# A mixing step on VectorE, late affine work on GpSimd, and the first step of each norm, in a two-block transformer kernel

## The chip, the cores and the metric

The kernel runs on one core of a Trainium2 chip, in one launch. The metric is the device time of the launch in microseconds (us), as the median of several runs; the time before is 1526.29 us. Inputs, weights and outputs are float32 in the chip's main memory.

The engines are called by short names: PE (matmuls), DVE (the vector engine), ACT (the scalar engine), POOL (GpSimd) and SP (used here for its queue of transfers).

## The reference

256 tokens of width 1024 pass two blocks. The part on which the change acts most is layer A of the first block:

```
proj = h @ w_in                       # 1024 -> 2 x 2048
u, gate = proj[..., :2048], proj[..., 2048:]
for g, w in enumerate((2, 4, 8, 16)): # 512 channels each
    cs = cumsum(u of group g over tokens)
    pooled = (cs - shifted(cs, w)) / min(pos + 1, w) - u of group g
    mixed = pooled @ w_grp[g]
y = (mixed * scale * silu(gate)) @ w_out
h = layer_norm(h * ALPHA + y) * ln_g + ln_b
```

Layer B of the same block makes keys and values from h, attends within dilated windows with 16 heads, gates, projects, and ends in a second layer norm. The second block has two layers, each with a token mixer and an MLP; each half ends with an rms norm of its output, a gated addition to the stream, and an rms norm of the stream for the next half, whose shift and scale come from a conditioning vector.

## The kernel before

**Products.** A float32 product is done as three PE matmuls on parts that were rounded to a narrower format: high by high, high by low, low by high (`mm3`, lines 178 to 183). Weights come in tiles of 512 KB (`stream`, L120 to L132): the SP queue loads `ws` (four buffers), ACT rounds it to the high part `wh` (L128), DVE subtracts to get the low part `wl` (L130); five buffers each. The activations are split in the same way by `split` (ACT L135, DVE L136). Tiles of activations hold features on the partitions and tokens along the row.

**Order.** The order of the matmuls on PE is written out by hand, with side work (`tick`, `weave`) put between the main ones; products for the conditioning (L268) serve as filling. On DVE, ACT, POOL and SP the order is set by a scheduler from priorities, in which later code comes later, and code under `high_priority(100)` is put ahead. Each engine then runs its own list strictly in that order.

**Layer A** (`layer_a`, L422 on). The tokens are transposed on PE (L432), then for each group of 512 channels, windows 16, 8, 4, 2 in turn, and for each half of a group (two feature tiles of 128): PE makes u; ACT copies it out (L457); DVE adds shifted copies, one to four times, to get the sum over the window (L462, tiles `wa` and `wb`); POOL multiplies by 1 / count (L465, constant `inv`) and subtracts u (L466); ACT and DVE split the result; then PE makes the gate half, and ACT and DVE its silu (L471, L472). The group's own product (`grp`, L493) stands one group behind. The output product follows (`out_mm`), and the two token tiles' layer norms: statistics on DVE (L539 to L542), `rstd`, normalising on DVE (L548). The normalised tiles are transposed on PE (`tile_T`, L377) and scaled while they are taken out (`hT_evac`, L400, L402).

**rstd** (L159 to L170) makes 1 / sqrt: a DVE step `v` (L164, or L166 in rms norms), then POOL's power (L169), which alone is under `high_priority(100)`. The rms norms end with DVE multiplying by it (L717 in `rms_tile`, L1075 in `residual`; L1071 and L1072 are the squares on ACT and the multiplication by the gate on DVE before it).

**The affine step.** The stream itself still needs ln_g and ln_b of layer A: eight POOL operations of 128x512 on `xt` in place (L604), for which `layer_b` keeps a list; two are given out behind each block of columns of layer B's values, six blocks (`cb`) in all, whose results are copied out of PSUM by DVE (L594) and ACT. They have no dependence on the values, so that they stand in POOL's list as soon as `xt` can be written, which is when the transposes have read it.

**Set-up** (L313 on). SP loads the identity, the two token tiles (128x1024 each, L323) and the first weights; DVE clears constants, among them S (L344).

## Time and profile before

| | before |
|---|---|
| median of 3 runs | 1526.29 us (1524.75 to 1528.28) |
| the profiled execution | 1525.75 us |
| its span | 1524.0 us |
| mean granted PE clock | 0.99 of full speed |
| busy: PE, DVE, ACT, POOL | 1469.2, 924.6, 721.2, 172.8 us |
| moved by DMA | 241.80 MB, 159 GB/s |

The span runs from the first to the last instruction; the 1.75 us between it and the execution's time lie outside. Engines run side by side, and each waits only where a tile is not yet there or not yet free. A share of busy time is an average over stages; what a wait costs is read where it stands, from the engine that has no work in hand. In the rows a `<-` behind an idle time names the instruction, or the transfer, that ended it.

### The profile page before, as it was taken

The page shows a single profiled execution, that of the slowest core. Times are in us where ns is not written, and L with a number is a line of the kernel's source. Part 1 is how long each engine was busy: PE and PEld are TensorE (multiplying, and loading weights), DVE is VectorE, ACT ScalarE, POOL GpSimd, SP SyncE. Part 2 cuts the span into 40 slices and gives each one's busy share as a digit, 9 for nine tenths or more (in the row PEclk, how much of TensorE's full clock was granted, in tenths as well). Part 3 has the DMA queues.
Part 4 walks back from the last instruction along what each step waited for, and adds up shares of the span by engine and source line. Part 5 has one row for each costly group of instructions (what it writes and reads, how often), then busy time and mean ns, then how long its engine had stood idle before and what let it go on. Part 6 is the DMA issues. An engine that isn't in the chain of part 4 may idle for free.

```text
span 1524.0 us, 23366 instructions
## 1 busy us (share of the span) xinstructions
PE 1469.2 (96%) x8966; PEld 1213.7 (80%) x8966; DVE 924.6 (61%) x1660; ACT 721.2 (47%) x1397; POOL 172.8 (11%) x240
## 2 busy tenths in 40 slices
PE   8899899999999999999899999999998999899998
PEld 8898678888999677776787777777886886599986
DVE  5676755657677877658774243433448687665554
ACT  4454444445466546645663232221426466555443
POOL 4431300000010142001100000000001220000000
PEclk9999999999999999999999999999999999999999
DMA  8568576867554722114434445343344255645562
GB/s 305 179 194 261 162 233 189 249 198 230 171 178 155 261 84 84 32 39 131 135 109 138 138 154 164 119 150 107 96 151 125 85 139 180 221 153 191 184 191 84
DMA packets 186544, 241.80 MB, mean 159 GB/s; under 512 B 15296, under 2 KB 132080, under 8 KB 186368
## 3 DMA queue, kind: packets, MB, share of 16 engines
q1 hardware_dynamic: 185168, 237.11, 49.4%
q0 software_dynamic: 1264, 3.19, 0.6%
q8 instruction: 70, 1.15, 0.3%
q14 instruction: 42, 0.34, 0.1%
HBM read 239.19 MB, written 2.03 MB: 158 GB/s over the span
## 4 chain that ended last, share of the span: by engine, by line
PE 68%; DVE 9%; POOL 4%; ACT 3%; issue 3%; DMA 1%; SPq 0%; POOLq 0%; DVEq 0%; ACTq 0%
PE ps L181 20%; PE ps L182 19%; PE ps L183 19%; POOL sm L169 2%; DVE wl L130 2%; PE ps L958 2%; PE ps L874 2%; PE ps L268 2%; PE ps L940 1%; PE ps L700 1%; PE ps L687 1%; POOL t L753 1%; DVE fm L136 1%; DVE sm L919 1%; PE ps L665 1%
## 5 line engine op out<-in xcount | busy, mean ns | idle before, releaser
L130 DVE TENSOR_TENSOR wl<-ws,wh 128x1024 fp32r<-128x1024 f32 x336 | 413.7, 1233 | 357.5 <-ACT wh L128 347.2
L128 ACT CAST wh<-ws 128x1024 fp32r<-128x1024 f32 x336 | 351.2, 1049 | 398.5 <-PE ps L183 211.7
L181 PE MATMUL ps<-fm,wh 128*128 128x256 f32 (+1 forms) x1416 | 428.2, 302 | 4.2 <-ACT fm L135 4.2
L183 PE MATMUL ps<-fm,wl 128*128 128x256 f32 (+1 forms) x1416 | 421.8, 298 | 5.0 <-DVE wl L130 4.9
L182 PE MATMUL ps<-fm,wh 128*128 128x256 f32 (+1 forms) x1416 | 421.6, 298 | 0.3 <-DVE fm L136 0.3
L182 PE MATMUL ps<-wl,fm 128*128 128x512 f32 (+1 forms) x912 | 355.6, 390 | 10.5 <-DVE wl L130 10.5
L181 PE MATMUL ps<-wh,fm 128*128 128x512 f32 (+1 forms) x912 | 364.0, 399 | 0.3 <-ACT fm L135 0.3
L183 PE MATMUL ps<-wh,fm 128*128 128x512 f32 (+1 forms) x912 | 354.8, 389 | 2.5 <-DVE fm L136 2.5
L181 PEld LDWEIGHTS ps<-fm,wh 128*128 128x128 f32 x1416 | 267.7, 189 | 30.5 <-issue 10.9
L183 PEld LDWEIGHTS ps<-fm,wl 128*128 128x128 f32 x1416 | 267.7, 189 | 15.6 <-DVE wl L130 6.7
L182 PEld LDWEIGHTS ps<-fm,wh 128*128 128x128 f32 x1416 | 267.6, 189 | 9.8 <-DVE fm L136 0.7
L181 PEld LDWEIGHTS ps<-wh,fm 128*128 128x128 f32 x912 | 172.4, 189 | 58.7 <-issue 17.7
L182 PEld LDWEIGHTS ps<-wl,fm 128*128 128x128 f32 x912 | 172.8, 189 | 48.3 <-DVE wl L130 14.0
L183 PEld LDWEIGHTS ps<-wh,fm 128*128 128x128 f32 x912 | 172.2, 189 | 42.7 <-DVE fm L136 4.2
L135 ACT CAST fm<-t 128x128 fp32r<-128x128 f32 (+2 forms) x232 | 85.5, 394 | 133.6 <-POOL t L466 50.8
L169 POOL TENSOR_TENSOR sm<-sm,mhalf 128x1 f32<-128x1 f32 (+3 forms) x42 | 39.4, 938 | 872.4 <-DVE sm L166 696.2
L136 DVE TENSOR_TENSOR fm<-t,fm 128x128 fp32r<-128x128 f32 (+2 forms) x232 | 90.2, 410 | 55.9 <-ACT fm L135 55.0
L923 ACT ACTIVATE e<-ps,sm 128x512 f32<-128x512 f32 (+1 forms) x96 | 59.3, 618 | 50.3 <-DVE sm L919 34.5
L919 DVE TENSOR_REDUCE sm<-ps 128x1 f32<-128x512 f32 (+1 forms) x96 | 55.9, 587 | 11.3 <-PE ps L1038 7.7
L1328 DVE SCALAR_TENSOR_TENSOR t<-ps,t 128x512 f32<-128x512 f32 (+1 forms) x64 | 35.3, 551 | 18.4 <-ACT t L1327 18.4
L1327 ACT ACTIVATE t<-ps 128x512 f32<-128x512 f32 (+1 forms) x64 | 31.2, 487 | 31.9 <-PE ps L183 31.9
L940 PE MATMUL ps<-ident,e 128*128 128x128 f32 x272 | 42.1, 274 | 2.6 <-ACT e L923 1.1
(203 smaller groups left out, 1217.0 us busy)
## 6 DMA issues: line engine op xcount, KB each, us to landing
ws<-in_w_mlp_in_dram SPq DMA_DIRECT2D x64, 512.0 KB, 3.8
ws<-in_w_mlp_out_dram SPq DMA_DIRECT2D x64, 512.0 KB, 3.7
mw<-in_w_mod_dram SPq DMA_DIRECT2D x48, 512.0 KB, 5.0
fm<-in_w_mod_dram SPq DMA_DIRECT2D x96, 256.0 KB, 5.4
ws<-in_w_kv_dram SPq DMA_DIRECT2D x48, 512.0 KB, 4.2
ws<-in_w_in_dram SPq DMA_DIRECT2D x40, 512.0 KB, 4.0
ws<-in_w_in_a_dram SPq DMA_DIRECT2D x32, 512.0 KB, 4.8
ws<-in_w_in_b_dram SPq DMA_DIRECT2D x32, 512.0 KB, 4.0
```

The costliest lines, as they stand in the source:

```text
L128: nc.scalar.copy(wh[:, :n], ws[:, :n])
L130: nc.vector.tensor_sub(wl[:, :n], ws[:, :n], wh[:, :n].bitcast(F32))
L135: self.nc.scalar.copy(hi, src)
L136: self.nc.vector.tensor_sub(lo, src, hi.bitcast(F32))
L169: self.pow = nc.gpsimd.tensor_tensor(r, v, self.mhalf[:, :n], op=ALU.pow)
L181: nc.tensor.matmul(ps, a[0], b[0], start=start, stop=False)
L182: nc.tensor.matmul(ps, a[0], b[1], start=False, stop=False)
L183: nc.tensor.matmul(ps, a[1], b[0], start=False, stop=stop)
L919: nc.vector.tensor_reduce(nm, ps[:, :n], axis=AX.X, op=ALU.max, negate=True)
L923: nc.scalar.activation(e, ps[:, :n], AF.Exp, bias=nm, accum_out=ss)
L940: nc.tensor.transpose(ps[:, k * 128:k * 128 + 128], e[:, k * 128:k * 128 + 128], self.ident)
L1328: nc.vector.scalar_tensor_tensor(q, p, 0.0, r, op0=ALU.max, op1=ALU.mult)
```

## The change

There are five edits.

1. In layer A, POOL's two operations for each of the 16 feature tiles become two on DVE: a multiplication of the first 16 tokens by a small table (`cut`, 128x16; the count differs from the window only there), and one operation that multiplies by 1 / window and subtracts u (128x256). The constant loaded for it on POOL's queue goes from 512 KB to 32 KB.
2. In layer B, POOL copies one column of the values' block, and only then runs the two affine operations given to that block. The copy reads what DVE writes in L594, so that it is a true wait, and the affine operations stand behind it in POOL's list.
3. In `rstd` the DVE step `v` is under `high_priority(100)` too.
4. The token tiles are loaded in four halves (first halves of both, then second halves), and four products of zeros run on PE before the first transposes, as soon as S is cleared.
5. A return value that nothing uses is gone.

```diff
-        v = self.sm(n)
-        if extra is None:
-            nc.vector.tensor_scalar(v, ss, scale, eps, op0=ALU.mult, op1=ALU.add)
-        else:
-            nc.vector.tensor_scalar(v, ss, eps, extra, op0=ALU.add, op1=ALU.add)
-        r = self.sm(n)
+        v, r = self.sm(n), self.sm(n)
         with self.tc.high_priority(100):
-            self.pow = nc.gpsimd.tensor_tensor(r, v, self.mhalf[:, :n], op=ALU.pow)
+            if extra is None:
+                nc.vector.tensor_scalar(v, ss, scale, eps, op0=ALU.mult, op1=ALU.add)
+            else:
+                nc.vector.tensor_scalar(v, ss, eps, extra, op0=ALU.add, op1=ALU.add)
+            nc.gpsimd.tensor_tensor(r, v, self.mhalf[:, :n], op=ALU.pow)
...
-        for t in range(2):
-            x = self.xtp.tile([128, 1024], F32, name="xt", tag="xt")
-            nc.sync.dma_start(x, I["x"][0, t * 128:(t + 1) * 128])
-            self.xt.append(x)
+        self.xt = [self.xtp.tile([128, 1024], F32, name="xt", tag="xt") for _ in range(2)]
+        for c in (0, 512):
+            for t in range(2):
+                nc.sync.dma_start(self.xt[t][:, c:c + 512], I["x"][0, t * 128:(t + 1) * 128, c:c + 512])
...
         nc.vector.memset(self.S, 0.0)
+        for _ in range(4):
+            nc.tensor.matmul(self.ps("M")[:, 0:256], self.S[:, 0:4].rearrange("p a b -> p (a b)"),
+                             self.S.rearrange("p a b -> p (a b)"), start=True, stop=True)
...
-            inv = pa.tile([128, 4, 256], F32, name="inv")
-            nc.gpsimd.dma_start(inv, I["inv_cnt"][0].partition_broadcast(128))
+            cut = pa.tile([128, 4, 16], F32, name="cut")
+            nc.gpsimd.dma_start(cut, I["cut"][0].partition_broadcast(128))
...
                         m = self.t1()
-                        nc.gpsimd.tensor_tensor(m, cur[:, 16:272], inv[:, g], op=ALU.mult)
-                        nc.gpsimd.tensor_tensor(m, m, u[:, 16:272], op=ALU.subtract)
+                        nc.vector.tensor_mul(cur[:, 16:32], cur[:, 16:32], cut[:, g])
+                        nc.vector.scalar_tensor_tensor(m, cur[:, 16:272], 0.5 ** (g + 1), u[:, 16:272],
+                                                       op0=ALU.mult, op1=ALU.subtract)
...
             if cb:
-                with self.tc.issue_after(i0.ins), self.tc.issue_after(i1.ins):
+                i2 = nc.gpsimd.tensor_copy(self.held, vt[0][cb][:, 0:1])
+                with self.tc.issue_after(i2.ins):
                     for _ in range(2):
                         if self.affine:
                             n, z, op = self.affine.pop(0)
                             nc.gpsimd.tensor_tensor(n, n, z, op=op)
```

Three places show what the change does to the engines' lists. Line numbers of the changed kernel are up to seven higher than those before (L604 is L611 there, L594 is L599, L717 is L724, L1072 and L1075 are L1079 and L1082, L130 is L131, L136 is L137, L166 is L168, L462 is L466).

POOL at the end of layer A, before: the affine step of the first token tile stands between the powers of the two layer norms.

```order
L466 TENSOR_TENSOR t_1498<-t_1498,u_185 128x256
L610 DMA dist<-in_dist_dram 128x1024
L169 TENSOR_TENSOR sm<-sm,mhalf 128x1
L604 TENSOR_TENSOR xt<-xt,gb 128x512 x4
L169 TENSOR_TENSOR sm<-sm,mhalf 128x1
L604 TENSOR_TENSOR xt<-xt,gb 128x512 x4
L801 TENSOR_TENSOR t_2547<-t_2545 128x128
```

The same place now (L606 is the copy of one column of the values):

```order
L617 DMA dist<-in_dist_dram 128x1024
L169 TENSOR_TENSOR sm<-sm,mhalf 128x1 x2
L808 TENSOR_TENSOR t_2560<-t_2558 128x128
L606 COPY held<-fm 128x1
L611 TENSOR_TENSOR xt<-xt,gb 128x512 x2
L606 COPY held<-fm 128x1
L611 TENSOR_TENSOR xt<-xt,gb 128x512 x2
```

The two powers now follow each other, and the affine operations come in pairs behind the copies, four pairs in all. On SP the loads of layer B's ln_g and ln_b, which reuse the buffers that the affine step reads, have moved back with them, behind the first four weights of the attention stage.

DVE in the first layer of the second block, at the norm between mixer and MLP, before:

```order
L136 TENSOR_TENSOR fm<-ps,fm 128x256
L1075 SCALAR_TENSOR_TENSOR fm<-t_8297,sm,fm 128x512
L1075 SCALAR_TENSOR_TENSOR fm<-t_8298,sm,fm 128x512
L166 TENSOR_SCALAR sm<-sm 128x1
L136 TENSOR_TENSOR fm<-ps,fm 128x256
L717 TENSOR_SCALAR t_8326<-fm,sm 128x512 x2
L136 TENSOR_TENSOR fm<-ps,fm 128x256
L130 TENSOR_TENSOR wl<-ws,wh 128x1024
L166 TENSOR_SCALAR sm<-sm 128x1
L136 TENSOR_TENSOR fm<-ps,fm 128x256
L717 TENSOR_SCALAR t_8336<-fm,sm 128x512 x2
L130 TENSOR_TENSOR wl<-ws,wh 128x1024
```

The same place now:

```order
L1079 TENSOR_TENSOR t_8314<-ps,gb 128x512
L1082 SCALAR_TENSOR_TENSOR fm<-t_8313,sm,fm 128x512
L168 TENSOR_SCALAR sm<-sm 128x1
L1082 SCALAR_TENSOR_TENSOR fm<-t_8314,sm,fm 128x512
L724 TENSOR_SCALAR t_8342<-fm,sm 128x512 x2
L137 TENSOR_TENSOR fm<-ps,fm 128x256
L168 TENSOR_SCALAR sm<-sm 128x1
L137 TENSOR_TENSOR fm<-ps,fm 128x256
L724 TENSOR_SCALAR t_8352<-fm,sm 128x512 x2
L137 TENSOR_TENSOR fm<-ps,fm 128x256 x2
L131 TENSOR_TENSOR wl<-ws,wh 128x1024 x3
```

The steps `v` stand further ahead, and the low parts of the weights that stood between and around the two scalings now come behind both.

DVE in layer A, first group, now (L469 and L470 are the new operations; before, an L462 stood where they do or nothing, and both L136 came behind the last `wl`):

```order
L469 TENSOR_TENSOR wb_199<-wb_199,cut 128x16
L131 TENSOR_TENSOR wl<-ws,wh 128x1024
L470 SCALAR_TENSOR_TENSOR t_292<-wb_199,u_193 128x256
L466 TENSOR_TENSOR wb_200<-wa_198 128x256
L131 TENSOR_TENSOR wl<-ws,wh 128x1024
L137 TENSOR_TENSOR fm<-t_292,fm 128x256
L469 TENSOR_TENSOR wb_200<-wb_200,cut 128x16
```

Low parts of weights stand between the steps of a feature tile's chain.

## Rows read from the trace of the kernel before

**Rows 1.** The page, first part: busy time, share of the span, instructions.
```profile
PE 1469.2 (96%) x8966; PEld 1213.7 (80%) x8966; DVE 924.6 (61%) x1660; ACT 721.2 (47%) x1397; POOL 172.8 (11%) x240
```

**Rows 2.** PE's waits over the span: us in total, times, longest.
```profile
PE ps L432 <- DMA xt<-in_x_dram: 5.8, 2, 5.0
PE ps L377 <- DVE t L717: 5.7, 4, 3.2
```

**Rows 3.** Groups by line, 20 to 170 us: busy, mean ns; idle before, its releaser.
```profile
L183 PE MATMUL ps<-fm,wl 128*128 128x256 f32 x296 | 83.2, 281 | 5.0 <-DVE wl L130 4.9
...
L130 DVE TENSOR_TENSOR wl<-ws,wh 128x1024 fp32r<-128x1024 f32 x52 | 63.8, 1231 | 20.1 <-ACT wh L128 18.9 <-PE ps L182 1.0
...
L465 POOL TENSOR_TENSOR t<-wb,inv 128x256 f32<-128x256 f32 x8 | 15.3, 1914 | 39.0 <-DVE wb L462 39.0
L466 POOL TENSOR_TENSOR t<-t,u 128x256 f32<-128x256 f32 x16 | 13.6, 848 | 1.2
...
L135 ACT CAST fm<-t 128x256 fp32r<-128x256 f32 x32 | 12.9, 407 | 57.3 <-POOL t L466 50.8 <-DVE t L501 6.6
...
L472 DVE SCALAR_TENSOR_TENSOR fm<-t,ps 128x256 f32<-128x256 f32 x16 | 6.5, 414 | 0.2 <-issue 0.2
```

**Rows 4.** Busy time by engine in layer A: length, then PE, PEld, DVE, ACT, POOL.
```profile
20.00:130.00 110.00, 103.94 (x872) 101.87 (x871) 76.40 (x126) 53.42 (x93) 46.49 (x48) 1.00 0.64 200
```

**Rows 5.** DVE's timeline, an operation of 128x16: start, us, line.
```profile
1330.48 0.17 DVE L298 TENSOR_TENSOR gc<-modc,V 128x16 f32<-128x16 f32 x1
```

**Rows 6.** POOL's timeline at the end of layer A: start, us, line [idle before].
```profile
177.28 5.15 POOL L604 TENSOR_TENSOR xt<-xt,gb 128x512 f32<-128x512 f32 x4 [3.58 <-PE ps L377]
182.39 0.55 POOL L169 TENSOR_TENSOR sm<-sm,mhalf 128x1 f32<-128x1 f32 x1
```

**Rows 7.** DVE's timeline there.
```profile
180.00 0.14 DVE L164 TENSOR_SCALAR sm<-sm 128x1 f32<-128x1 f32 x1
...
189.61 2.29 DVE L130 TENSOR_TENSOR wl<-ws,wh 128x1024 fp32r<-128x1024 f32 x1
```

**Rows 8.** PE's timeline there.
```profile
183.58 1.97 PE L377 MATMUL ps<-ident,xt 128*128 128x128 f32 x8 [3.24 <-DVE xt L548]
...
192.26 0.49 PE L183 MATMUL ps<-wh,fm 128*128 128x512 f32 x1 [2.47 <-DVE fm L136]
```

**Rows 9.** Four stretches: columns as in rows 4, then granted clock, DMA share, GB/s.
```profile
184.00:188.00 4.00, 4.00 (x18) 1.85 (x16) 4.00 (x10) 2.15 (x8) 3.22 (x2) 0.50 0.00 0
192.00:196.00 4.00, 3.47 (x8) 2.23 (x9) 4.00 (x11) 2.00 (x6) 0.00 (x0) 0.60 0.90 352
200.00:250.00 50.00, 50.00 (x216) 40.30 (x215) 26.29 (x25) 22.60 (x26) 0.46 (x1) 1.00 0.65 205
780.00:784.00 4.00, 3.64 (x20) 3.65 (x21) 3.97 (x16) 3.14 (x13) 0.00 (x0) 0.59 0.01 3
```

**Rows 10.** PE's timeline at the norms of the second block.
```profile
757.83 0.50 PE L182 MATMUL ps<-wl,fm 128*128 128x512 f32 x1 [1.89 <-DVE wl L130]
758.17 0.39 PE L183 MATMUL ps<-wh,fm 128*128 128x512 f32 x1
...
780.36 1.97 PE L377 MATMUL ps<-ident,t 128*128 128x128 f32 x8 [3.15 <-DVE t L717]
...
1158.11 0.50 PE L182 MATMUL ps<-wl,fm 128*128 128x512 f32 x1 [2.92 <-DVE wl L130]
```

**Rows 11.** DVE's timeline before PE's 780.36, the operations that waited for POOL's power.
```profile
773.74 0.88 DVE L717 TENSOR_SCALAR t<-xt,sm 128x512 f32<-128x512 f32 x2 [0.44 <-POOL sm L169]
...
776.67 1.41 DVE L1075 SCALAR_TENSOR_TENSOR xt<-t,sm,xt 128x512 f32<-128x512 f32 x2 [0.73 <-POOL sm L169]
...
779.81 0.88 DVE L717 TENSOR_SCALAR t<-xt,sm 128x512 f32<-128x512 f32 x2 [0.47 <-POOL sm L169]
```

**Rows 12.** DVE's timeline at the program's end.
```profile
1517.89 0.69 DVE L1072 TENSOR_TENSOR t<-ps,gb 128x512 f32<-128x512 f32 x1 [2.02 <-ACT t L1071]
1518.50 0.20 DVE L166 TENSOR_SCALAR sm<-sm 128x1 f32<-128x1 f32 x1
```

More of the change, by code (lines that the diff above doesn't have):

```diff
@@ L26, in host_constants @@
     t = np.arange(256)
-    inv = np.stack([1.0 / np.minimum(t + 1, w) for w in (2, 4, 8, 16)]).astype(np.float32)
-    c["inv_cnt"] = inv.reshape(1, 4, 256)
+    cut = np.stack([w * (1.0 / np.minimum(t[:16] + 1, w)).astype(np.float32) for w in (2, 4, 8, 16)])
+    c["cut"] = cut.astype(np.float32).reshape(1, 4, 16)
     p = np.arange(128)
@@ L319, in setup @@
         nc.gpsimd.tensor_copy(self.identr, self.ident)
-        self.xt = []
-        for t in range(2):
-            x = self.xtp.tile([128, 1024], F32, name="xt", tag="xt")
-            nc.sync.dma_start(x, I["x"][0, t * 128:(t + 1) * 128])
-            self.xt.append(x)
+        self.xt = [self.xtp.tile([128, 1024], F32, name="xt", tag="xt") for _ in range(2)]
+        for c in (0, 512):
+            for t in range(2):
+                nc.sync.dma_start(self.xt[t][:, c:c + 512], I["x"][0, t * 128:(t + 1) * 128, c:c + 512])
         rows = self.cst.tile([80, 128], F32, name="rows")
@@ L337, in setup @@
                 nc.gpsimd.dma_start(rows2[r:r + 8], I["norm_g_2"][l, 1 + 2 * w].rearrange("(r c) -> r c", c=128))
+        self.held = self.cst.tile([128, 1], F32, name="held")
         self.mhalf = self.cst.tile([128, 8], F32, name="mhalf")
@@ L480, in layer_a @@
         order = [g * 4 + i for g in (3, 2, 1, 0) for i in range(4)]
-        ns, pw = self.out_norm(I["w_out_a"][0], order, self.act256(yh, yl), 0)
+        ns = self.out_norm(I["w_out_a"][0], order, self.act256(yh, yl), 0)
         def norm_T(t):
@@ L567, in out_norm @@
         self.lng = (g, b)
-        return ns, self.pow
+        return ns
     def layer_b(self):
```

## The prediction

> **What bounds the kernel.** I read the page first: PE is busy for 96% of the span [rows 1], so that time can be won only where PE waits, or where its clock is low. Then PE's waits over the span, and the groups by line of the first 170 us, for the places; then the timelines of PE, DVE and POOL around each, to see what ended last; then stretches of a few us, for the granted clock. The reader is to see three kinds of place. At the start PE waits 5.8 us for the tokens [rows 2]. In layer A PE has 103.94 of 110 us [rows 4], and most of the 6.06 us that it lacks are waits for low parts of weights, 4.9 us from 20 to 170 [rows 3], behind which POOL stands, as shown below. At the norms PE waits for the normalised tile: longest at the end of layer A (3.24 and 2.47 us [rows 8]) and in the second block (3.15 us [rows 10]).
>
> All sums are made against the profiled execution, 1525.75 us, 0.54 us below the median 1526.29. Some 0.2%, 3 us, is what a measurement of this kernel can tell from no change.
>
> **Layer A's mixing step.** Removed are 16 multiplications and 16 subtractions on POOL; where the window's sum is in `wb`, which is eight tiles, they take 1.91 + 0.85 = 2.76 us one behind the other [rows 3]. ACT's split waits for them, 50.8 us in total [rows 3], and since ACT works its list in order, the rounding of the next weight stands behind that wait, DVE's low part behind the rounding, and PE behind the low part: 4.9 us. Added are 16 operations of 128x16 and 16 of 128x256 on DVE. Neither is in the trace; the nearest rows are an operation of 128x16 at 0.17 us [rows 5] and one of the same kind and size at 0.414 us [rows 3]. I take these: 0.58 us for a tile, 9.3 us in all, and a chain shorter by 2.2 us in the eight tiles. DVE goes from 76.4 to 85.7 of 110 us [rows 4]. The first group is the tight one: for each half PE has four weights of 24 matmuls, at 103.94 / 872 = 0.119 us each [rows 4] 11.4 us, and DVE four low parts at 1.23 and twice seven operations of 0.41 and one of 0.17, 11.1 us. Later groups have one sum less each, and more PE work. So most of the 6.06 us goes and some stays: I take 4.8, with 1 (each wait keeps most of its length behind DVE's longer list) and 5.8 as ends. The smaller constant on POOL's queue I cost at nothing: PE lacks nothing before the first group's sums are made.
>
> **The affine step held back.** At the end of layer A the step `v` of the second norm ends at 180.14, but its power starts at 182.39, the moment POOL is done with four affine operations [rows 6, 7]: 2.25 us. PE starts the second tile's transposes at 183.58 [rows 8]. With POOL free I put the power at 179.6 to 180.2 (DVE's work beside POOL shrinks too: the low part at 189.61 took 2.29 us there, against 1.23 [rows 3, 7]) and the transposes at 180.85, so that PE idles some 0.5 us instead of 3.24. After the long idle PE ran at the lower level, 0.50 of full speed from 184 to 188 [rows 9]; without it the transposes, eight fillers and five products, which took from 183.58 to 189.79, take half, 3.1 us, and end at 184.0. PE then waits for DVE's splits, 2.2 us instead of 2.47, and goes on at 186.2 instead of 192.26 [rows 8]: 6.05 us. What follows ran at 0.60 in 192 to 196 [rows 9]; that may stay or go, 0 to 2.5 us, because 2.2 us lies between an idle of 1.89 that left the next matmul at 0.39 us [rows 10] and one of 3.24 that did not [rows 8, 9]. I take the middle, 1.25: **7.3 us** (5 to 8.7).
>
> What the step collides with next: eight affine operations, two for a block, lie among layer B's values, where PE is busy 50 of 50 us, DVE 26.3, POOL 0.5 [rows 9]. A low part beside such an operation lost 1.06 us [rows 3, 7]; eight of them would be 8.5 us, and DVE has 23.7 idle there. Zero. The copies of one column, 0.55 us each by the power, which is of that size [rows 6], wait on an idle POOL for one block of values each; behind them stands only work for the attention stage. The loads of layer B's ln_g and ln_b move back on SP, past four weights; they are used at layer B's end. Zero, and the weights no longer stand behind a load that waits for the affine step (no transfers at all from 184 to 188 [rows 9]).
>
> **The step `v` ahead.** It is 0.2 us on DVE, but POOL's power and DVE's next operation hang on it. In the second block, DVE waited for three powers before PE's 780.36: 0.44, 0.73 and 0.47 us [rows 11]. With `v` ahead, the power runs beside other DVE work. Following DVE's list by hand with the old durations gives the scaling at 777.95 instead of 779.81: PE idles 1.3 instead of 3.15 us [rows 10]. An idle of that length left the clock up at 757.83 [rows 10], where it fell at 780.36; the stretch from 780 to 784 at 0.59 [rows 9] gives back 4 x 0.41 = 1.65: **3.5 us** (1.9 to 3.5). At the norm before, three low parts now come behind both scalings; the third is ready at 757.0 instead of 757.7: 0.5 us (-0.8 to 0.7). After the first MLP PE waits 2.92 us for a low part [rows 10]; there the first low part moves ahead of the norm's steps, the second stands half a microsecond further back, and the third is ready earlier: 0.9 us (-0.5 to 2). The other three waits for L717 are 5.7 - 3.15 = 2.55 us [rows 2, 10]; I take a third, 0.8 (0 to 1.2). At the very end `v` stood behind a multiplication that started at 1517.89 [rows 12] and now stands ahead of it: 0.6 us.
>
> **Start.** PE needs tokens, not clears. Before, all 16 transposes need whole tiles; now the first half of them needs half the bytes. And the zeros run while PE would wait, on a constant that DVE clears first, so that the clock may be up for the transposes. The trace shows no such early work: bound 0 (the weights set the pace, or the clock is low as before) and 1.5 us; I take 1.0, nearer to the top because PE's waits at the start are for the tokens [rows 2]. The matmuls of zeros themselves lie inside that 5 us.
>
> **Sum.** 1.0 + 4.8 + 7.3 + 0.5 + 3.5 + 0.9 + 0.8 + 0.6 = 19.4; 1525.75 - 19.4 = 1506.3; on the median's scale **1507 us**.
>
> **Rivals.**
> (1) DVE becomes layer A's bound: PE's waits stay, 1507 + 4.8 = 1512, or in part the new 9.3 us come on the path, to 1521. For it: 11.1 of 11.4 us in the first group. Against it: 24 us of slack over the stretch, and up to five low parts in hand.
> (2) The clock is lost anyway: 2.2 us of idle after layer A lowers it, and 1.3 us before 780 does so too. Then 1.25 and 1.65 are not won, nor part of the half-speed stretch, and the time is 1510. For it: idles of 3.15 and 3.24 us stand before slow stretches [rows 8 to 10]; against it: 1.89 does not [rows 10]. [...]
> (3) Slower: in layer A the chain of both tiles of a half stands in DVE's list, in order, before the next low part. If DVE has none in reserve, PE idles for 2 x (0.17 + 0.41 + 0.41 for ACT's split + 0.41) = 2.8 us in each of eight halves, and an idle of that length costs clock too (1.65 us at 780): 8 x 4.4 = 36, on top of the lost 4.8: 1547 us. It decides when DVE falls behind by its reserve, five weights of 2.86 us of PE's work, 14 us. Against it: DVE's surplus work is 9.3 us in all, and low parts stand between the steps in the new list.
> (4) The change doesn't do what it says: if the affine operations find their copy done early, or the powers still come late, the end of layer A keeps its 7.3 us: 1514.
>
> **How the numbers follow.** Forecast 0.61; rival 1 0.15; rival 2 0.12; rival 3 0.03; rival 4 0.05; several of 1, 2 and 4 together with the small terms at their lower ends, which is a gain below 3 us, 0.04. Faster by over 0.2% is all but the last and rival 3: 0.93; the same 0.04; slower 0.03. With all terms at their upper ends the time is 1502, and 1500 leaves room for waits that shrink further down; at the top 1518 takes in rivals 2 and 4 and most of 1. Left out are some 0.16.
>
> **What would show it.** In the changed kernel's trace: POOL nearly idle from 20 to 170 us, and PE's waits for low parts there below 1.5 us together; the power of layer A's second norm directly behind its `v`; an idle of PE below 1 us before the second transposes, and matmuls at full pace behind them; affine pairs among the values at 205 to 245 with no wait of PE; the wait before the transposes near 770 below 2 us and no slow stretch behind. Wrong would be: new waits of PE for low parts in the first group, DVE without idle time in layer A, or slow rows after idles of 2 us or less.

## The result, and the profile after

The changed kernel takes 1507.77 us (median of 4 runs, 1507.59 to 1509.51), against 1526.43 us for the kernel before on the same chip: a ratio of 0.988, with a 95% interval of 0.9863 to 0.9897. That is 18.7 us, faster by clearly more than 0.2%; 1507 was forecast. The profiled execution took 1507.9 us with a span of 1506.1, 17.8 us less than before (before rounding). So the total came out within a microsecond. Its terms did not: two missed by 3 us each, in opposite directions.

The page's first part, and PE's waits over the span (the columns are those of [rows 1] and [rows 2]):

```profile
PE 1466.6 (97%) x8974; PEld 1213.5 (81%) x8974; DVE 927.7 (62%) x1692; ACT 723.5 (48%) x1397; POOL 136.0 (9%) x213
```

```profile
PE ps L182 <- DVE wl L131: 10.4, 8, 4.0
PE ps L181 <- ACT fm L136: 5.0, 4, 2.4
...
PE ps L381 <- DVE t L724: 2.2, 2, 1.4
...
PE ps L181 <- ACT wh L129: 1.7, 1, 1.7
...
PE ps L436 <- DMA xt<-in_x_dram: 1.1, 1, 1.1
...
PE ps L183 <- DVE wl L131: 0.8, 1, 0.8
```

PE's work is what it was, and the waits at L183, L377 (now L381) and for the tokens have shrunk. New is a wait for the high part `wh`. The longest wait for a low part has grown, from 2.9 to 4.0 us.

**Where the time came from.** PE runs the same matmuls in the same order in both kernels; the changed one has only the zeros ahead (8 records). So the n-th matmul after them can be laid beside the n-th of before, and the difference of their starts is what has been won up to there. The first of the second token tile's transposes, for instance, starts at 183.58 before [rows 8] and at 175.45 after (a row below): 8.13 us. At stage ends:

| matmul before at, us | after at | won so far | by the stage | forecast |
|---|---|---|---|---|
| 20.11, first weights | 22.40 | -2.29 | start -2.3 | 1.0 (0 to 1.5) |
| 130.03, mixing done | 124.74 | 5.29 | layer A 7.6 | 4.8 (1 to 5.8) |
| 200.21, first values | 188.49 | 11.72 | its end 6.4 | 7.3 (5 to 8.7) |
| 740.13 | 728.55 | 11.58 | -0.1 | 0.8 with the later norm |
| 757.83 | 745.41 | 12.42 | 0.85 | 0.5 |
| 790.08 | 774.53 | 15.55 | 3.1 | 3.5 |
| 1180.04, after the MLP | 1164.09 | 15.94 | 0.4 | 0.9 |
| 1345.10, second layer | 1327.96 | 17.13 | 1.2 | in the 0.8 above |
| end of the span, 1524.0 | 1506.1 | 17.8 | 0.7 | 0.6 |

The table is of one execution of each kernel. The profiles of the experiments below show which of its rows repeat: in all that leave the place as it is in the changed kernel, layer A gives 7.58 us, its end 6.42 to 6.46, and the stretch from 740 to 790 us 3.97 to 4.24. The start and the place after the MLP do not repeat: six profiles with the start of the changed kernel lose 2.3 to 3.1 us there, and after the MLP 0.4 to 1.7 us are won.

**The start** (timelines of PE, of ACT and of SP's queue of loads: start, us, line [idle before]; then a stretch as in [rows 9]):

```profile
1.21 3.78 PE L347 MATMUL ps<-S 128*128 128x256 f32 x8 [1.21 <-DVE S L344]
4.78 1.56 PE L436 MATMUL ps<-ident,xt 128*128 128x128 f32 x8
7.42 1.44 PE L436 MATMUL ps<-ident,xt 128*128 128x128 f32 x8 [1.08 <-DMA xt<-in_x_dram]
10.55 0.38 PE L181 MATMUL ps<-fm,wh 128*128 128x256 f32 x1 [1.69 <-ACT wh L129]
```

```profile
9.46 1.04 ACT L129 CAST wh<-ws 128x1024 fp32r<-128x1024 f32 x1 [2.45 <-DMA ws<-in_w_in_a_dram]
```

```profile
1.17 1.84 SPq L323 DMA_DIRECT2D xt<-in_x_dram  x4
```

```profile
12.00:16.00 4.00, 4.00 (x22) 4.00 (x22) 3.81 (x5) 2.81 (x4) 0.92 (x10) 0.57 0.87 168
```

Before, the same two rows of ACT and SP were:

```profile
7.81 1.05 ACT L128 CAST wh<-ws 128x1024 fp32r<-128x1024 f32 x1
```

```profile
1.17 0.89 SPq L323 DMA_DIRECT2D xt<-in_x_dram  x2
```

The transposes are quick, as hoped (1.56 and 1.44 us for eight each; before, 3.25 for the last 14). But the second halves come late, and the first weight later still: ACT waits for it until 9.46, and after PE's waits of 1.08, 1.69 and (for a low part) 0.76 us the clock is low from 12.5 to 16 (0.57 of full speed in the row from 12 to 16). Of the 2.29 us, 1.19 are lost by PE's first weight product (10.55 against 9.37) and 1.10 from there to 20 us.

**Layer A** (groups from 20 to 170 us, as [rows 3]; then the stretch of [rows 4]):

```profile
L136 ACT CAST fm<-t 128x256 fp32r<-128x256 f32 x32 | 12.3, 404 | 11.3 <-DVE t L470 10.9 <-DVE t L506 0.3
...
L470 DVE SCALAR_TENSOR_TENSOR t<-wa,u 128x256 f32<-128x256 f32 x8 | 3.4, 425 | 0.2
...
L469 DVE TENSOR_TENSOR wa<-wa,cut 128x16 f32<-128x16 f32 x8 | 1.4, 175 | 0.3
```

```profile
20.00:130.00 110.00, 110.00 (x921) 109.32 (x920) 93.88 (x180) 62.31 (x104) 7.61 (x16) 1.00 0.76 234
```

PE has no wait left: 110 of 110 us, on 921 matmuls where it did 872 before. ACT's idle time before its splits fell from 57.3 to 11.3 us, and the two new operations took 0.175 and 0.42 us, as estimated. DVE's 93.88 us can't be set beside the 76.40 of before, because the stretch now holds more of the program; over the same 910 matmuls DVE went from 84.5 to 94.6 us, 10.1 more where 9.3 were worked out.

**The end of layer A** (POOL, PE, and a stretch):

```profile
174.27 0.55 POOL L169 TENSOR_TENSOR sm<-sm,mhalf 128x1 f32<-128x1 f32 x1 [5.85 <-DVE sm L166]
```

```profile
175.45 1.11 PE L381 MATMUL ps<-ident,xt 128*128 128x128 f32 x8 [0.39 <-DVE xt L553]
...
178.76 0.50 PE L181 MATMUL ps<-wh,fm 128*128 128x512 f32 x1 [1.20 <-ACT fm L136]
```

```profile
180.00:184.00 4.00, 2.75 (x9) 1.08 (x8) 4.00 (x10) 2.42 (x7) 0.00 (x0) 1.00 0.87 317
```

The 3.24 us of idle are 0.39, the clock stays at 1.00, and instead of one wait of 2.47 us PE has four small ones, 2.4 us together.

**The affine step among the values** (POOL, one pair of four, and its second operation alone; DVE beside it; the stretch that answers to the third of [rows 9]):

```profile
204.26 0.19 POOL L606 COPY held<-fm 128x1 f32<-128x1 f32 x1 [26.54 <-DVE fm L599]
204.41 3.64 POOL L611 TENSOR_TENSOR xt<-xt,gb 128x512 f32<-128x512 f32 x2
```

```profile
205.78 2.26 POOL L611 TENSOR_TENSOR xt<-xt,gb 128x512 f32<-128x512 f32 x1
```

```profile
205.66 1.23 DVE L131 TENSOR_TENSOR wl<-ws,wh 128x1024 fp32r<-128x1024 f32 x1 [1.46 <-ACT wh L129]
```

```profile
193.00:243.00 50.00, 50.00 (x216) 40.30 (x215) 25.68 (x25) 21.30 (x24) 14.86 (x12) 1.00 0.68 207
```

PE is busy throughout, and the low part beside POOL took its usual 1.23 us. POOL's second operation, which started 0.12 us after it, took 2.26 us instead of 1.29.

**The second block** (PE):

```profile
743.14 0.50 PE L182 MATMUL ps<-wl,fm 128*128 128x512 f32 x1 [1.24 <-DVE wl L131]
...
766.18 1.09 PE L381 MATMUL ps<-ident,t 128*128 128x128 f32 x8 [1.41 <-DVE t L724]
...
1142.95 0.80 PE L182 MATMUL ps<-wl,fm 128*128 128x512 f32 x1 [4.01 <-DVE wl L131]
```

The wait of 3.15 us is 1.41 (1.3 was worked out), and the transposes behind it take 1.09 us instead of 1.97 [rows 10]. After the MLP one wait of 4.01 has taken the place of three, 0.7, 2.92 and 0.59 us.

### The profile page after: what moved, and what is told of

Read it like the earlier page. It is cut to its first block, busy times and chain, and to the rows that moved or that the text cites. A ratio compares the mean times of both kernels' runs of the same rounds, so it can differ in the third digit from the quotient of the medians.

```text
span 1506.1 us, 23366 instructions
## 1 busy us (share of the span) xinstructions
PE 1466.6 (97%) x8974; PEld 1213.5 (81%) x8974; DVE 927.7 (62%) x1692; ACT 723.5 (48%) x1397; POOL 136.0 (9%) x213
## 4 chain that ended last, share of the span: by engine, by line
PE 42%; DVE 4%; ACT 2%; issue 1%; POOL 1%; DMA 0%; POOLq 0%; DVEq 0%; SPq 0%; ACTq 0%
PE ps L181 13%; PE ps L182 13%; PE ps L183 13%; DVE wl L131 1%; PE ps L965 1%; PE ps L268 1%; POOL sm L169 1%; PE ps L947 1%; POOL t L760 0%; ACT fm L136 0%; PE ps L881 0%; ACT t L404 0%; ACT t L1078 0%; DVE t L724 0%; DVE xt L1082 0%
## 5 line engine op out<-in xcount | busy, mean ns | idle before, releaser
L131 DVE TENSOR_TENSOR wl<-ws,wh 128x1024 fp32r<-128x1024 f32 x336 | 411.8, 1227 | 369.8 <-ACT wh L129 359.7
L183 PE MATMUL ps<-fm,wl 128*128 128x256 f32 (+1 forms) x1416 | 421.5, 298 | 0.8 <-DVE wl L131 0.8
L183 PE MATMUL ps<-wh,fm 128*128 128x512 f32 (+1 forms) x912 | 354.5, 389 | 1.0 <-DVE fm L137 0.9
L183 PEld LDWEIGHTS ps<-fm,wl 128*128 128x128 f32 x1416 | 267.6, 189 | 10.0 <-DVE wl L131 1.0
L181 PEld LDWEIGHTS ps<-wh,fm 128*128 128x128 f32 x912 | 172.1, 189 | 59.4 <-issue 17.8
L183 PEld LDWEIGHTS ps<-wh,fm 128*128 128x128 f32 x912 | 172.1, 189 | 40.7 <-DVE fm L137 2.3
L136 ACT CAST fm<-t 128x128 fp32r<-128x128 f32 (+2 forms) x232 | 85.2, 394 | 85.0 <-DVE t L1335 41.9
L137 DVE TENSOR_TENSOR fm<-t,fm 128x128 fp32r<-128x128 f32 (+2 forms) x232 | 87.5, 399 | 28.5 <-ACT fm L136 27.4
L926 DVE TENSOR_REDUCE sm<-ps 128x1 f32<-128x512 f32 (+1 forms) x96 | 56.1, 589 | 11.3 <-PE ps L1045 7.7
L1335 DVE SCALAR_TENSOR_TENSOR t<-ps,t 128x512 f32<-128x512 f32 (+1 forms) x64 | 35.4, 553 | 18.7 <-ACT t L1334 18.7
```

The source lines that it names most:

```text
L131: nc.vector.tensor_sub(wl[:, :n], ws[:, :n], wh[:, :n].bitcast(F32))
L136: self.nc.scalar.copy(hi, src)
L137: self.nc.vector.tensor_sub(lo, src, hi.bitcast(F32))
L181: nc.tensor.matmul(ps, a[0], b[0], start=start, stop=False)
L183: nc.tensor.matmul(ps, a[1], b[0], start=False, stop=stop)
L926: nc.vector.tensor_reduce(nm, ps[:, :n], axis=AX.X, op=ALU.max, negate=True)
```

## The experiments

Twelve kernels were run, on several chips, each beside the kernel before. Times are compared as differences of the medians, kernel before minus this one: 18.7 us for the changed kernel in its first measurement, 18.85 in a second one (the last experiment but three). What a kernel loses or gains against the changed one is reckoned from the middle of the two, 18.75, and in the last three from 18.85, which was measured on the chip of the next two. The first eight are the changed kernel with something undone or altered; the last three try to better its start or the place after the MLP.

### Whole token tiles

```diff
-        for c in (0, 512):
-            for t in range(2):
-                nc.sync.dma_start(self.xt[t][:, c:c + 512], ...)
+        for t in range(2):
+            nc.sync.dma_start(self.xt[t], I["x"][0, t * 128:(t + 1) * 128])
```

> The changed kernel with its token tiles loaded whole again (two loads of 128x1024); the products of zeros stay. Theory A (the halves lose the start): in the changed kernel SP issues four token loads in 1.84 us instead of two in 0.89, so the first weight is rounded at 9.46 instead of 7.81 us, and PE's first weight product starts at 10.55 instead of 9.37. With whole tiles the first rounding is back at about 7.8 us, PE's first weight product starts at 8.9 to 9.4, and the time is 2 to 3 us below the changed kernel: about 1505.3 us. Theory B (the zeros lose it, because they hold PE until 4.99 us and use up the clock): no more than 0.7 us below the changed kernel, 1507 or above.

Measured: 1506.25 us, ratio 0.9864 (0.9849 to 0.9879), 20.8 us won, 2.1 more than the changed kernel. ACT's first rounding:

```profile
8.40 1.04 ACT L129 CAST wh<-ws 128x1024 fp32r<-128x1024 f32 x1 [0.85 <-DMA ws<-in_w_in_a_dram]
```

PE's first weight product is at 9.50. Theory A holds for the time, at the lower end of its range; the rounding did not come back to 7.8, nor the product to 9.4.

### No zeros

```diff
-        for _ in range(4):
-            nc.tensor.matmul(self.ps("M")[:, 0:256], ..., start=True, stop=True)
```

> The changed kernel without its products of zeros; the halves stay. Theory A: PE waits for the weights anyway (first rounding at 9.46 us), so the zeros only set the clock; without them the first 3 to 6 us of weight products run at the lower level, as they did from 12.5 to 15.9 with them: within 0.8 us of the changed kernel, 1507.0 to 1508.6. Theory B: the zeros delay the transposes: 1.5 to 2.5 us below the changed kernel, 1505.3 to 1506.3.

Measured: 1509.01 us, ratio 0.988 (0.9863 to 0.9896), 18.05 won: 0.7 worse than the changed kernel. The zeros do not delay the transposes (without them the first starts at 4.86, with them at 4.78). What they bring with the halves is too little to tell from nothing: both ratios are 0.988.

### The start as before

Both edits undone.

> The changed kernel with both start edits undone (whole tiles, no zeros). By the comparison of PE's n-th matmul in the two traces the start has lost 2.29 us by 20 us. Theory A and B both give those back: 1505.5 us (1504.8 to 1506.2), PE's first weight product at 9.37. If that loss is only where the clock's level happened to change in the two profiled runs, the time stays at 1507.8 within 0.5.

Measured: 1506.32 us, ratio 0.9865 (0.985 to 0.9879), 20.7 won, the same as with the zeros on whole tiles. So the halves cost 2.1 to 2.7 us and the zeros bring nothing that shows once the tiles are whole. One caution: with the same code as before at the start, this profile stood 1.4 us behind the kernel before by 20 us, because tokens and weights happened to land later (PE went on with the transposes at 6.89 against 6.46, and ACT started the first rounding at 8.66 against 7.81). Of the 2.29 us, then, an unknown part is the two executions' luck; the medians carry the verdict. More profiles agree with them: by 20 us, six with halves stand 2.3 to 3.1 us behind the kernel before, and two with whole tiles and zeros 1.25 us behind and 0.34 ahead.

### The mixing step back on POOL

```diff
-                        nc.vector.tensor_mul(cur[:, 16:32], cur[:, 16:32], cut[:, g])
-                        nc.vector.scalar_tensor_tensor(m, cur[:, 16:272], 0.5 ** (g + 1), u[:, 16:272], ...)
+                        nc.gpsimd.tensor_tensor(m, cur[:, 16:272], inv[:, g], op=ALU.mult)
+                        nc.gpsimd.tensor_tensor(m, m, u[:, 16:272], op=ALU.subtract)
```

> The changed kernel with the mixing step back on POOL (multiplication by 1/count and subtraction, with the 512 KB constant); all else stays. Theory A (the chain through POOL held ACT's list, and with it the low parts): the 7.57 us that PE's n-th matmul gained between 45 and 140 us are lost again, 1515.3 us (1514.0 to 1516.5), with five to eight waits of PE for low parts between 40 and 130 us. Rival: the freed time comes mostly from the smaller constant and the changed order at the start of the layer, so that less than 4 us are lost, below 1512.

Measured: 1514.35 us, ratio 0.9917 (0.9903 to 0.9932), 12.7 won, 6.0 less than the changed kernel. The stretch of [rows 4], and PE's waits in it:

```profile
20.00:130.00 110.00, 104.67 (x880) 102.92 (x879) 75.71 (x126) 52.24 (x92) 44.49 (x48) 1.00 0.67 207
```

```profile
PE ps L183 <- DVE wl L131: 2.7, 4, 0.8
PE ps L181 <- ACT wh L129: 1.5, 1, 1.5
PE ps L181 <- ACT fm L136: 1.0, 1, 1.0
```

The waits are back and the time with them, though those for low parts are four and not five to eight. By PE's n-th matmul this kernel wins only 0.85 us in layer A instead of 7.58. The edit also brings back the larger constant; but all that the new step wins by the n-th matmul is won after 45 us, so that a slower load at the start is not what it undoes.

### A busy POOL beside the new mixing step

```diff
+                        dm = pa.tile([128, 256], F32, name="dm", tag="dm", bufs=2)
+                        nc.gpsimd.tensor_tensor(dm, u[:, 16:272], u[:, 16:272], op=ALU.mult)
+                        nc.gpsimd.tensor_tensor(dm, dm, u[:, 16:272], op=ALU.subtract)
```

> The changed kernel with work for POOL put back beside the mixing step: for each feature tile a multiplication of u by itself and a subtraction of u, 128x256, into a tile that nothing reads (32 operations more than needed). Theory of the chain (POOL's place in the chain cost the time, not its being busy): within 1.2 us of the changed kernel, 1506.6 to 1509.0, and DVE's operations of 128x256 stay at 0.42 us. Theory of the contention (a busy POOL slows DVE, and DVE at 94 of 110 us has no room): DVE's operations grow beyond 0.5 us, waits of PE for low parts come back, 4 us or more lost, above 1511.8.

Measured: 1508.23 us, ratio 0.9881 (0.9866 to 0.9896), 18.6 won: nothing lost. But DVE did slow down (groups from 20 to 170 us, then the stretch):

```profile
L466 DVE TENSOR_TENSOR wa<-u 128x256 f32<-128x256 f32 x16 | 10.7, 670 | 0.0
```

```profile
20.00:130.00 110.00, 110.00 (x923) 109.41 (x922) 105.40 (x180) 60.32 (x103) 40.65 (x47) 1.00 0.74 232
```

The sums take 0.67 us instead of 0.42, and DVE is busy 105 of 110 us; PE still never waits. So in layer A it was POOL's place in the chain that cost the time, and not its being busy. A rival had DVE as the next bound at 9.3 us of added work; it carried 11.5 us more than that.

### The affine step not held back

```diff
-                i2 = nc.gpsimd.tensor_copy(self.held, vt[0][cb][:, 0:1])
-                with self.tc.issue_after(i2.ins):
+                with self.tc.issue_after(i0.ins), self.tc.issue_after(i1.ins):
```

> The changed kernel without the copies that hold the affine step back: POOL's list has four affine operations between the two powers again. By PE's n-th matmul the end of layer A gained 6.44 us, so the theory (the second power stood behind four affine operations, and the lower clock behind that wait) expects 6 to 6.9 us more than the changed kernel: 1514.2 us, with an idle of PE above 3 us before the second transposes and half-speed matmuls behind it. Rival: layer A's faster mixing has moved the end of the layer so that the collision is smaller: under 4 us, below 1511.8.

Measured: 1516.0 us, ratio 0.993 (0.9915 to 0.9945), 10.8 won: 7.9 lost, more than expected; 7.35 of it at the end of layer A by PE's n-th matmul. PE's timeline there:

```profile
179.07 1.11 PE L381 MATMUL ps<-ident,xt 128*128 128x128 f32 x8 [3.24 <-DVE xt L553]
...
187.73 0.79 PE L183 MATMUL ps<-wh,fm 128*128 128x512 f32 x1 [2.94 <-DVE fm L137]
```

The late power costs its 2.85 us before these transposes; they run at full pace (1.11 us; before, 1.97 [rows 8]) behind the same idle of 3.24. The other 4.5 us are lost behind them.

### The affine step held only until the second norm is done

```diff
-                i2 = nc.gpsimd.tensor_copy(self.held, vt[0][cb][:, 0:1])
+                i2 = nc.gpsimd.tensor_copy(self.held, self.xt[1][:, 0:1])
```

> The changed kernel with the affine step held back only until the second token tile is normalised (the copy reads that tile, not the values): the two powers stay together, but POOL runs its eight operations beside DVE's splits and low parts at 176 to 190 us, and PE's first weights of layer B. Theory of the order (only the late power cost time): nothing is lost, below 1509.0. Theory of the contention (the splits and low parts beside POOL cost as much: one low part took 2.29 us there instead of 1.23): PE's six small waits behind the transposes grow to over 3 us together, and the clock may fall; 2 to 5 us lost, 1510 to 1513.

Measured: 1517.74 us, ratio 0.9943 (0.9926 to 0.9959), 9.1 won: 9.7 us lost, outside both expectations and worse than not holding it at all. DVE, and PE:

```profile
175.89 4.84 DVE L137 TENSOR_TENSOR fm<-t,fm 128x128 fp32r<-128x128 f32 x5
180.65 1.04 DVE L406 TENSOR_SCALAR t<-ps,V 128x128 f32<-128x128 f32 x3
```

```profile
175.58 1.12 PE L381 MATMUL ps<-ident,xt 128*128 128x128 f32 x8 [0.39 <-DVE xt L553]
...
182.09 0.57 PE L181 MATMUL ps<-wh,fm 128*128 128x512 f32 x1 [4.41 <-ACT fm L136]
...
186.44 0.80 PE L183 MATMUL ps<-wh,fm 128*128 128x512 f32 x1 [2.07 <-DVE fm L137]
```

The power is on time and the transposes start as early as in the changed kernel (0.39 us of idle). Then five splits on DVE beside POOL take 4.84 us instead of 1.64, and PE waits 4.41, 2.07 and 1.11 us and stays at the lower clock (0.50 of full speed from 184 to 192). A late power is not needed for the loss; POOL beside DVE's splits is enough.

### The step `v` out of the priority

```diff
-        with self.tc.high_priority(100):
-            if extra is None:
+        if extra is None:
...
+        with self.tc.high_priority(100):
             nc.gpsimd.tensor_tensor(r, v, self.mhalf[:, :n], op=ALU.pow)
```

> The changed kernel with the DVE step of each norm out of the priority again (POOL's power keeps it). By PE's n-th matmul the places where it moved gained 0.85 + 3.1 in the first layer of the second block, 0.4 after its MLP, 0.55 in the second layer and 0.7 at the end, 5.6 us in all: 1513.4 us (1512.2 to 1514.6), with the wait of some 3 us and the slow stretch behind it back at about 766 us. Rival: the gains there come from another place of the low parts in DVE's list that the scheduler found by chance, and come back in part elsewhere: less than 3 us, below 1510.8.

Measured: 1514.71 us, ratio 0.992 (0.9905 to 0.9935), 12.1 won: 6.6 lost, at the upper end of what was expected. The four runs spread from 1511.4 to 1516.1, and the profiled one is the fastest. There the wait before the transposes is back to the hundredth:

```profile
768.33 1.09 PE L381 MATMUL ps<-ident,t 128*128 128x128 f32 x8 [3.15 <-DVE t L724]
```

but the transposes behind it ran at full pace (1.09 us; before, 1.97 [rows 10]), and the clock fell only later (0.68 of full speed from 768 to 772). The profiled run loses 3.5 us to the changed kernel's first profile: 3.3 between 200 us and the last matmul and 0.6 behind it, less 0.4 by which its own start and layer A were better. The three slower runs have no trace, but a mean granted clock of 0.990 to 0.991 where the profiled one has 0.993. So part of what `v` wins is idle time, and part is clock, in some executions.

### The changed kernel once more

> The changed kernel itself, on the chip on which the next two run, so that they can be compared: 18.7 us below the kernel before, as first measured (18 to 19.5); profiles of it may differ at the start and after the first MLP by one or two us, where waits of 1 to 4 us lower the clock in some executions and not in others.

Measured: 1508.03 us, ratio 0.9878 (0.9863 to 0.9892), 18.85 won.

### Second token tile from ACT's queue

Whole tiles, and:

```diff
-            nc.sync.dma_start(x, I["x"][0, t * 128:(t + 1) * 128])
+            (nc.sync, nc.scalar)[t].dma_start(x, I["x"][0, t * 128:(t + 1) * 128])
```

> The changed kernel with whole token tiles, of which the second is loaded from ACT's queue and the first from SP's, so that SP issues the first weight one load earlier. If the issue on SP is what delays the first weight (0.47 us for a load), its rounding starts 0.3 to 0.6 us earlier than with both whole tiles on SP (8.40 us), and the time is 0.3 to 0.8 us below that kernel, 2.5 to 3.3 below the changed one. If the transfers themselves are the limit (the DMA engines were busy at 1.07 of their share from 6 to 12 us there), nothing is won against whole tiles: 1.5 to 2.3 us below the changed kernel.

Measured: 1505.88 us, ratio 0.9865 (0.985 to 0.9879), 21.0 won, 2.15 more than the changed kernel on the same chip. ACT's first rounding:

```profile
7.77 1.05 ACT L129 CAST wh<-ws 128x1024 fp32r<-128x1024 f32 x1 [0.16 <-DMA ws<-in_w_in_a_dram]
```

It is 0.63 us earlier than with both on SP, and in the next kernel, with both on SP again, it is at 8.35, so the issue does matter. The time does not show it: 2.15 us lies in the range that was given for no gain over whole tiles, and the step from 20.8 to 21.0 is too small to tell from nothing.

### Two low parts put ahead after the MLP

Whole tiles on SP, and the first two weights of the second layer's first product:

```diff
-        nc.vector.tensor_sub(wl[:, :n], ws[:, :n], wh[:, :n].bitcast(F32))
+        p = self.wprio.pop(0) if self.wprio else 0
+        with self.tc.high_priority(p):
+            nc.vector.tensor_sub(wl[:, :n], ws[:, :n], wh[:, :n].bitcast(F32))
...
     def layer1(self):
+        self.wprio = [150] * 2
```

> The changed kernel with whole token tiles on SP, and with the low parts of the first two weights of the second block's second layer put ahead on DVE (priority), so that the second of them stands in front of the two L1082 of the norm and not behind them. PE's wait of 4.0 us for that low part (after the first MLP, at 1143 us) should fall by the 1.4 us of the two operations, and the slow stretch behind it may shorten: 1 to 2.5 us below whole tiles alone, 3 to 4.8 below the changed kernel. Rival: the norm that is put back is waited for in its turn: no gain over whole tiles.

Measured: 1504.46 us, ratio 0.9857 (0.984 to 0.9874), 22.4 won, 3.6 more than the changed kernel. PE's wait went from 4.01 to 2.98 us (line numbers are four higher in this kernel):

```profile
1139.26 0.80 PE L186 MATMUL ps<-wl,fm 128*128 128x512 f32 x1 [2.98 <-DVE wl L135]
```

From 1150 to 1180 us this kernel wins 1.50 us by PE's n-th matmul. Of ten profiles with the wait of 4.0 us, six win 0.4 to 1.0 us there and four 1.64 to 1.66. So the edit gives no more than an execution without it can have; that it gives the better outcome more often is not shown by two profiles.

### Both of the last two

> Both of the last two edits together: the second token tile from ACT's queue, and the two low parts put ahead. They lie 1100 us apart, so the gains should add: against the kernel before, 21.0 us (queue) and 22.4 us (low parts), with 20.6 us for whole tiles alone, gives 22.8 us, a ratio near 0.985 and about 1504.1 us; below 1505 if they add, and above 1505.5 if the earlier start is lost again later.

Measured: 1505.54 us (its kernel before 1527.93), ratio 0.9851 (0.9837 to 0.9864), 22.4 won. No more than with the low parts alone, so adding is not shown, nor a loss. The profile with ACT's queue alone is one of the four that win 1.65 us after the MLP anyway; here that place gives 1.54. Either version beats the kernel before by 22.4 us and the changed kernel by some 3.6.

## Why the prediction was right, and where its steps were wrong

**What bounds the kernel: right.** All that was won was won where PE waited or its clock was low.

**Layer A: right mechanism, term too small (4.8, measured 7.58 by PE, 6.0 by undoing it).** The failed step is how the waits were added up. The idle time of a row counts from the end of the matmul before, and matmuls overlap (0.28 us each, 0.12 us apart). A wait of the kernel before:

```profile
45.19 0.28 PE L182 MATMUL ps<-fm,wh 128*128 128x256 f32 x1
46.09 0.38 PE L183 MATMUL ps<-fm,wl 128*128 128x256 f32 x1 [0.62 <-DVE wl L130]
46.31 0.28 PE L181 MATMUL ps<-fm,wh 128*128 128x256 f32 x1
```

Without waiting, a matmul of 128x256 starts 0.12 us after the one before it (43.90, 44.01, 44.13 in this trace). Here 0.90 and then 0.22 us pass: 0.88 us lost, where the row says 0.62. Seven such waits, 5.8 of the 6.06 us that PE lacked [rows 4], make some 7.7 with 0.26 more for each, and the part that I held back for waits that stay was not needed: none stayed. The worry behind it, DVE's 11.1 of 11.4 us in the first group, was no limit; that low parts in hand carried even the busy POOL is likely, but was not tried by itself.

**The end of layer A: the size was right (6.4 for 7.3), the cause was named too narrowly.** I put the gain on the power that stood behind four affine operations, and on the clock. The trace of before fits that, with 2.25 us of waiting, and 2.85 of the 6.44 us are won before the second transposes start. The other 3.6 are won behind them. With the power on time and the affine step beside the splits the kernel loses 9.7 us. So the change wins here also by taking POOL's 128x512 operations away from a place where DVE has no gap (4.00 of 4 us from 184 to 188 [rows 9]) and PE waits for DVE; how much of the 3.6 is this and how much the clock was not separated. I had priced that contention from one row, the low part of 2.29 us [rows 7], and only for the values, where I expected 1.06 us for each operation and found none: there the low part stays at 1.23, and it is POOL's operation behind it that takes longer, 2.26 us instead of 1.29 [rows 6]. The zero for that place was right, but not for the reason given for it.

**The step `v` ahead: right in place and size in the trace.** 0.85 and 3.1 us against 0.5 and 3.5; the idle of 1.41 against 1.3; the clock kept up behind it (1.00 from 768 to 772). At the end 0.7 against 0.6. After the first MLP 0.4 against 0.9, and 0.4 to 1.7 over the ten profiles with that order, inside the stated -0.5 to 2: the reordering merged three waits into one of 4.01 us, and the kernel without `v` ahead gained 2.0 us at that place (its waits are 0.69, 2.92 and 1.33).

**The start: wrong (1.0, measured -2.3 in the trace and about -2 by undoing the halves).** The failed step is "PE needs tokens, not clears": I priced the halves by what PE gains when the first arrive, and counted nothing for the queue that they are moved ahead of. SP issues a load in some 0.46 us; four instead of two (1.84 against 0.89 us) push every weight 0.95 us back, and the weight, not the tokens, ended PE's last wait before its first product. Of the 1.65 us by which the first rounding came later, whole tiles bring back 1.06. My lower bound of 0 had no reason behind it: an edit that adds two issues ahead of a critical load can lose. Before, ACT rounded the first weight right behind its first split, at 7.81; in the kernel with the same start (The start as before) it waited 0.46 us for it, so that the weight had little slack to give.

**The rivals.** The third, the slower one, and the first fell with the layer without waits; the fourth fell with the power that starts right behind its `v` and the affine pairs behind their copies. The second, that the clock is lost anyway, did not hold at 180 and at 766 us (1.00 of full speed from 180 to 184 and from 768 to 772); the clock was lost at the start and after the MLP instead (0.57 from 12 to 16, 0.50 from 1144 to 1149). Where it falls differs between executions. The changed kernel's matmul behind 4.01 us of idle (the row at 1142.95) takes 0.80 us; with the start of before it is:

```profile
1143.66 0.50 PE L182 MATMUL ps<-wl,fm 128*128 128x512 f32 x1 [4.03 <-DVE wl L131]
1144.00 0.56 PE L183 MATMUL ps<-wh,fm 128*128 128x512 f32 x1
1144.36 0.63 PE L181 MATMUL ps<-wh,fm 128*128 128x512 f32 x1
```

In one the lower level (0.63 us for a matmul of 128x512, against 0.39 at full speed) is there at once, in the other two matmuls later. By PE's n-th matmul that place gives 0.4 us in the one and 1.6 in the other. What sets that place was not shown.

**The sum.** 1506.3 was worked out for a profiled execution and 1507.9 measured; start and layer A were off by -3.3 and +2.8 us. That the forecast lies so near is partly luck; the wait accounting was too small by about as much as the start was too good.

## What to carry to other kernels

Before moving or splitting a load, count its issues on its queue (some 0.46 us each here), and look at which load stands behind it and who waits for that one. When an engine that shares work with another gets free, ask not only what waits for its result but beside which operations it runs, and which of them starts first: here the same eight operations cost 9.7 us beside a chain that PE waited for, and nothing beside work with gaps. To add up PE's waits, compare starts of matmuls with their usual distance (0.12 us for 128x256 here) rather than summing the idle times of rows.

## What the runs showed of the hardware that was not expected

Side by side, POOL's operations of 128x512 and DVE's splits and low parts took longer, and in the four places below it was chiefly the one that started second. Two pairs of rows show it. The first is from the kernel whose affine step is held only until the second norm is done, the second from the one whose affine step is not held back:

```profile
175.99 1.45 POOL L611 TENSOR_TENSOR xt<-xt,gb 128x512 f32<-128x512 f32 x1
```

```profile
176.21 1.49 DVE L137 TENSOR_TENSOR fm<-t,fm 128x128 fp32r<-128x128 f32 x1
```

```profile
179.38 1.62 DVE L137 TENSOR_TENSOR fm<-t,fm 128x128 fp32r<-128x128 f32 x5
```

```profile
179.81 2.32 POOL L610 TENSOR_TENSOR xt<-xt,gb 128x512 f32<-128x512 f32 x1 [1.38 <-DVE fm L137]
```

In the first, POOL's operation is under way when the split starts, and the split ends 0.26 us after POOL's. Three of the five splits are held so, 1.45 to 1.49 us each, and the five take 4.84 us. In the second the same five splits are under way when POOL's operation starts; they take 1.62 us, against 1.64 in the changed kernel, and POOL's takes 2.32 us instead of 1.29. Among the values the low part starts first and keeps its 1.23 us, and POOL's second operation takes 2.26. The kernel before shows the other side there: its low part of 2.29 us [rows 7] started at 189.61, while a POOL operation ran from 189.40 to 190.82. Not every DVE operation pays: three L406, which read their tile from PSUM, took 1.04 us beside POOL's 128x512 and 1.06 in the changed kernel, where none of these ran.

With POOL kept busy through layer A, DVE's sums of 128x256 grew from 0.42 us to means of 0.56 to 0.67. In the kernel before their means were 0.42 to 0.43 with POOL almost as busy (46.5 of 110 us [rows 4], against 40.7). What ran side by side differs. In the kernel before POOL's work waited for those very sums, and 6 of the 39 sums in the trace lay beside a POOL operation; four of these took 0.42, the others 0.51 and 0.55. With the added work 25 of 40 did; these took 0.75 us on the mean, the other 15 took 0.42.
